# The last four up tiles of an MLP's first quarter as two seven-product pairs, with the sums of x made by ScalarE and GpSimd

## The chip, the core and the metric

One core of a Trainium2 chip runs the whole program. The metric is the device time of one execution in microseconds (us). The engines are named as in the profile: PE (TensorE, matrix products; PEld is its weight load), DVE (VectorE), ACT (ScalarE), POOL (GpSimd) and SP (SyncE, which here only issues DMAs). Each engine works through its instructions in order; semaphores tie the engines together.

## The reference

A two-layer encoder on 576 tokens (512 of a prompt, 64 of a running stream) with a model width of 1024. Layer 0 mixes tokens by causal pooling, layer 1 by sparse attention; each is followed by a squared-ReLU MLP.

```python
def _mlp(h, w_up, w_down):
    u = jax.nn.relu(h @ w_up)          # 1024 -> 4096
    return (u * u) @ w_down            # 4096 -> 1024
...
x = x + y                              # pooling or attention
x = x + _mlp(_rmsnorm(x, norm_mlp[i]), mlp_w_up[i], mlp_w_down[i])
```

## The kernel before, in words

Everything is fp32 to the reader of its output, but PE works on two-part numbers: a value is split into a high part (a cast by ACT to fp32r) and a low part (the difference, mostly by DVE), and a product is high·high + high·low + low·high, three matmuls. Activations lie as `x[k]`, k = 0 to 7, 128 features by 576 tokens each; a matmul takes one half of the tokens, 288 (`HT`).

**An MLP** (`mlp`, once for each layer) runs in four quarters c of the inner 4096 features. A quarter makes eight up tiles (1024 to 128 features each) and then four Down pairs, which add the quarter's part of the result to `x`. The norm's factor 1/rms isn't multiplied into the input: it is needed only where an up tile leaves PSUM (`rb`; the tile is called `rbm` in the first layer), so PE can begin before the norm is known. The steps of the norm: ACT squares `x[k]` (L343), DVE sums the squares (L344), PE sums over features (`st`), ACT and DVE make 1/rms with small steps (L396 to L403), DVE writes it on a diagonal (L366, L369), PE spreads it (`rb`, L356) and ACT copies it (L357). PE has the diagonal's two matmuls in the middle of plain tile 2.

**Plain tiles.** In the first quarter all eight up tiles are plain: `project` (L326) takes 48 matmuls for one, 8 k × 2 halves × 3, with two units of weights, `wh` and `wl` of 128x512 each. `finished` takes the tile out: DVE applies ReLU and `rbm` into the v tile (L480), ACT squares (L472), and then sums for the Down pairs' seven products are made (L502 to L515) and split into u, high by ACT (L491), low by DVE (L494). There is one v tile (`v_tile`, bufs=1).

**Seven-product pairs.** In the quarters 1 to 3 up tiles are made in pairs, `Up`, and Downs always are. `seven` computes a 2 by 2 block product with seven products instead of eight: products t1 to t4, b11, b21, b22 of 12 matmuls each (`product`, L528), 84 for two up tiles where plain ones would take 96. They go to three PSUM banks a, b and c in the order b11, t1, t2, b21, t3, b22, t4, and the scheduler may move some of them past another. `act.copy(a_, b)` (L565) copies b11 to a second bank. The products need sums of the weights (`sum`, by accumulating DMAs of POOL, L235 and L256, and by DVE, L281 and L285) and sums of x, called `xt`: three per j (t1, t2, t4), j = 0 to 3, each from `x[j]` and `x[half + j]`, and they need `xs[j]` replaced by a difference for `b22` and the like (`x_difference`).

**Sums of x before the change.** `x_sums(j, ...)` (L445) takes one ACT scaling of 128x288, four DVE operations of 128x288 (L451 to L454), an ACT cast and a DVE low part of 128x864. It is called after plain tile 3 for j = 0 and after tile 5 for j = 1; j = 2 and 3, and the `x_difference`s, come beside the first Downs (`x_prepared`).

**Weights.** `Stream` loads raw weights by SP's queue into a few raw tiles, in the order of the list `jobs`; a raw tile is loaded anew when the low part of what it held has been made. An "even" and an "odd" block belong to a pair; loading an odd one adds the even one to it by an accumulating DMA on POOL's queue. `units` yields split units one after another, and `ahead` sets how far it runs before PE.

**Seeds.** In the first four calls of `seven` of each MLP a further matmul writes `a_` before the copy overwrites it (`SEEDED`, L564). Nothing reads its result.

**The order of the instructions.** The code is written in the order of the work; a scheduler then fixes each engine's sequence, and within an engine nothing passes a waiting instruction. The changed kernel's line numbers are a little off those of before: L193/L194 are the same, L235, L256, L316, L326, L344, L357, L480 and L528 of before are L237, L258, L318, L328, L346, L359, L483 and L531.

Of the kernel before, what the change touches and what calls it, by code (L numbers as in the profile page):

```python
# [49 lines left out]
SPARE_UNITS = 6  # L50
RAWS = (4, 3)
MLP_BLOCKS = ("up", "even", "odd", "down")
SEEDED = 4
LEAD = 5
UP_ORDER = (0, 4, 1, 5, 2, 6, 3, 7)
FACTORS = ("t4", "t3", "t1", "t2", "b11", "b22", "b21")
FIRST_DOWN = (0, 2, 1, 3)

# [2 lines left out]
def pool_dsa_kernel(ctx: ExitStack, tc: tile.TileContext, a, o):  # L61
# [61 lines left out]
    def f32(t):  # L123
        return t.bitcast(F32)
# [37 lines left out]
    def mlp_jobs(layer, plain=0):  # L162
        for c in range(4):
            for n, f in enumerate(UP_ORDER):
                kind = "odd" if c and n % 2 else "even" if c else "up"
                jobs.append((kind, a["w_up"][layer, c * 8 + f], KT * P))
            for m in range(KT) if c else [2 * q + i for q in FIRST_DOWN for i in range(2)]:
                kind = "down" if c == 3 and m >= KT - plain else "odd" if m % 2 else "even"
                jobs.append((kind, a["w_down"][layer, c, m], KT * P))
# [27 lines left out]
    class Stream:  # L197
# [13 lines left out]
        def fill(self):  # L211
            while jobs:
                kind, src, n = jobs[0]
                mlp = kind in MLP_BLOCKS
                room = self.room(mlp)
                if room is None:
                    return
# [200 lines left out]
    def mlp(layer, gi, late=0, end=None):  # L418
# [23 lines left out]

            return (KT - LAST if end and c == 3 else KT) // 2

        def x_sums(j, raw, first, difference):  # L445

            t = x_sums_tile()
            xt.append(t)
            gain, minus = gv[:, gi, j:j + 1], negative[:, half + j:half + j + 1]
            act.activation(first, x[j][:, :HT], AF.Copy, scale=gain)  # L450
            dve.scalar_tensor_tensor(raw[:, 0], x[j][:, HT:], gain, first, ALU.mult, ALU.subtract)  # L451
            dve.scalar_tensor_tensor(difference, x[half + j][:, :HT], gv[:, gi, half + j:half + j + 1], first, ALU.mult, ALU.subtract)
            dve.scalar_tensor_tensor(raw[:, 1], x[half + j][:, :HT], minus, raw[:, 0], ALU.mult, ALU.subtract)
            dve.scalar_tensor_tensor(raw[:, 2], x[half + j][:, HT:], minus, raw[:, 1], ALU.mult, ALU.subtract)  # L454
            act.copy(t[:, :, 0], raw)
            dve.tensor_tensor(t[:, :, 1], raw, f32(t[:, :, 0]), ALU.subtract)

        def x_difference(j, difference):

            split(xs[j][:, :, :HT], difference)  # L460

        def of_x(j, factor, part):
            if factor[0] == "b" or factor == "t3":
# [32 lines left out]
        def parts_of(u, v, f):  # L496

            upper(u, v, f)
            return lower(u, v, f)
# [29 lines left out]
                                    skip_group_check=True)  # L529
            return ins  # L530

        tasks = [0]
        parted = []
        gates = []
        left = []
# [17 lines left out]
        def seven(operand, late, on):  # L553
# [5 lines left out]
            w = take()  # L559
            with behind([parted.pop()] if parted else []):  # L560
                product(b, w, operand, "b11", rows, True)
            tasks[0] += 1
            if tasks[0] <= SEEDED:
                pe.matmul(a_[:, :HT], w[0][:, :P], operand(0, "b11", 0), start=True, stop=True, skip_group_check=True)  # L564
            act.copy(a_[:, :HT], b[:, :HT])  # L565
            ahead()
            w1 = take()
# [143 lines left out]
        def finished(i, pt, us):  # L711
            nonlocal pair
            if i % 2 == 0:
                pair = tiles()
            v, u = pair
            activated(pt, v[:, 5:7] if i % 2 else v[:, 1:5:3])
            if i == KT - 2:
                parts_of(u, v, slice(4, 5))
                first_sum(v)
                parts_of(u, v, slice(2, 3))  # L720
            elif i == KT - 1:
                middle_sums(v)
                parts_of(u, v, slice(1, 4, 2))
                upper(u, v, slice(5, 7))
                last_sum(v)
                lower(u, v, slice(5, 7))
                parts_of(u, v, slice(0, 1))
            elif i % 2:
                upper(u, v, slice(4, 7))
                first_sum(v)  # L730
                middle_sums(v)
                last_sum(v)
                upper(u, v, slice(0, 4))
                lower(u, v, slice(4, 7))
                lower(u, v, slice(0, 4))
            if i % 2:
                us.append(u)

        todo, us = [], []
        for i in range(KT):  # L740
            w = next_block()
            pt = (psum1("up"), psum1("up")) if i == 2 else psum("up")
            project(pt, w, xs, spread() if i == 2 else iter(()))
            todo.append((i, pt, us))
            if i == 1:
                norm.stats()
            if i < 2:
                continue
            for t in todo:
                finished(*t)  # L750
            todo.clear()
            if i in (3, 5):
                r = 2 * i - 6
                if i == 3:
                    snap = halves(tmp("snap", "s2", 1))
                x_sums(i // 2 - 1, rough[:, r:r + 3], rough[:, r + 3], snap[:, i // 2 - 1])

        def x_prepared(n):

            if n < 2:  # L760
                v = v_tile()
                x_difference(n, snap[:, n])
                x_sums(n + 2, v[:, :3], v[:, 3], v[:, 4])
                x_difference(n + 2, v[:, 4])

        for n, q in enumerate(FIRST_DOWN):
            seven(of(us), n == 0, Down(q))
            x_prepared(n)
        for c in range(1, 4):
            us = []  # L770
            for j in range(half):
# [930 lines left out]
```

## Time and profile before

| | |
|---|---|
| median of three runs | 1071.51 us (1071.14 to 1071.96) |
| the profiled execution | 1070.67 us |
| its span, first to last instruction | 1068.8 us |
| mean granted clock of PE | 0.997 |
| busy: PE / DVE / ACT / POOL | 1046.4 / 912.0 / 625.7 / 239.5 us |
| layer 0, pooling and the plain tiles' start | plain tile 0 begins at 41.4 us |
| layer 1's MLP | its first tiles run at 680 us |

A row of the timeline gives the start, the duration, the engine, the line, the operation, what it writes and reads, its shape, how often it is repeated without a gap, and in brackets how long the engine was idle before it and what ended that. A row of groups gives the count, the busy time and the mean of one in ns, then the idle time before these instructions. A row of windows gives the busy time of PE, PEld, DVE, ACT and POOL with counts, then the clock, the DMA engines' share and GB/s. DVE's and ACT's instructions overlap a little, the next starting some 0.07 to 0.1 us before the last one's end.

### The profile page before, as it was taken

Reading aid. Unit: us, or ns where it says so; the run is one execution under the profiler, and the core shown is the slowest. Engines: PE = TensorE matmul, PEld = TensorE weight load, DVE = VectorE, ACT = ScalarE, POOL = GpSimd, SP = SyncE. Lnnn points to the kernel's source line nnn. Section 1 sums busy time; section 2 is a strip of 40 time slices with the busy share of each in tenths; the row PEclk is TensorE's granted clock in tenths of the full one; section 3 lists DMA queues with packets and bytes.
Section 4 is the critical chain, followed back from the end, with each engine's and each line's share of the span. In section 5 each row is a group of like instructions: output and inputs, shape, how many; then the busy total and the mean of one; then the engine's idle time right before and its main releaser. Section 6 shows DMA issues by size and latency. Waiting matters only on the chain.

```text
span 1068.8 us, 21707 instructions
## 1 busy us (share of the span) xinstructions
PE 1046.4 (98%) x7978; PEld 1022.7 (96%) x7978; DVE 912.0 (85%) x1865; ACT 625.7 (59%) x1252; POOL 239.5 (22%) x254
## 2 busy tenths in 40 slices
PE   8999999999999999999999999999999999999996
PEld 8999999999999999999999888999999999999995
DVE  7879989879988998889999675689889879979974
ACT  8556457547646765454368776456457447547742
POOL 3200111111111110667546620000111111111101
PEclk9999999999999999999999999999999999999998
DMA  8233666676576665845552554343666676676522
GB/s 254 89 102 92 165 165 163 158 179 156 151 182 169 157 173 176 237 137 139 170 156 75 169 170 107 126 107 89 178 159 149 178 172 164 149 183 163 124 55 89
DMA packets 98027, 159.65 MB, mean 149 GB/s; under 512 B 15697, under 2 KB 29312, under 8 KB 97920
## 3 DMA queue, kind: packets, MB, share of 16 engines
q1 hardware_dynamic: 70720, 111.78, 33.2%
q0 software_dynamic: 15840, 28.84, 17.1%
q10 hardware_dynamic: 11360, 17.63, 5.1%
q8 instruction: 63, 1.03, 0.4%
q14 instruction: 44, 0.36, 0.1%
HBM read 142.99 MB, written 12.72 MB: 146 GB/s over the span
## 4 chain that ended last, share of the span: by engine, by line
PE 84%; DVE 7%; DMA 3%; issue 2%; POOL 2%; ACT 1%; SPq 0%; ACTq 0%; DVEq 0%; POOLq 0%
PE b L528 33%; PE c L528 16%; PE up L326 9%; PE a L528 8%; PE pj L326 4%; PE wo L326 2%; PE wa L326 2%; PE pb L1072 1%; PE pt L1402 1%; PE dn L326 1%; PE o L1434 1%; DVE mask L1319 1%; PE sc L1376 1%; DVE m L1318 1%; DMA raw<-in_w_in 1%
## 5 line engine op out<-in xcount | busy, mean ns | idle before, releaser
L193 ACT CAST wh<-raw 128x512 fp32r<-128x512 f32 x308 | 189.7, 620 | 208.5 <-PE b L528 65.9
L194 DVE TENSOR_TENSOR wl<-raw,wh 128x512 fp32r<-128x512 f32 x284 | 198.2, 700 | 33.6 <-ACT wh L193 29.5
L528 PE MATMUL b<-u,wh 128*128 128x288 f32 x992 | 203.3, 296 | 2.3 <-ACT a L565 1.9
L528 PEld LDWEIGHTS b<-u,wh 128*128 128x128 f32 x992 | 159.6, 188 | 4.3 <-ACT a L565 3.1
L193 ACT CAST wh<-sum 128x512 fp32r<-128x512 f32 x165 | 102.3, 620 | 95.7 <-PE b L528 41.6
L528 PE MATMUL b<-u,wl 128*128 128x288 f32 x496 | 145.9, 295 | 0.4 <-DVE wl L194 0.4
L194 DVE TENSOR_TENSOR wl<-sum,wh 128x512 fp32r<-128x512 f32 x165 | 112.2, 686 | 22.3 <-ACT wh L193 20.8
L256 POOL DMA_DIRECT2D sum<-in_w_down x31 | 27.1, 894 | 340.9 <-DMA sum<-in_w_down 102.5
L528 PE MATMUL c<-u,wh 128*128 128x288 f32 x496 | 102.7, 296 | 0.0
L528 PEld LDWEIGHTS b<-u,wl 128*128 128x128 f32 x496 | 93.5, 189 | 0.6 <-DVE wl L194 0.6
L326 PE MATMUL up<-xs,wh 128*128 128x288 f32 x512 | 89.6, 296 | 0.9 <-DVE x L1593 0.8
L494 DVE TENSOR_TENSOR u<-v,u 128x576 fp32r<-128x576 f32 (+3 forms) x106 | 83.0, 786 | 2.0 <-ACT u L491 1.6
L528 PEld LDWEIGHTS c<-u,wh 128*128 128x128 f32 x496 | 79.8, 188 | 1.3 <-ACT wh L193 1.1
L528 PE MATMUL b<-xt,wh 128*128 128x288 f32 x384 | 77.7, 296 | 0.0
L528 PE MATMUL b<-xs,wh 128*128 128x288 f32 x384 | 77.2, 295 | 0.0
L326 PEld LDWEIGHTS up<-xs,wh 128*128 128x128 f32 x512 | 74.6, 188 | 2.0 <-ACT wh L193 1.0
L491 ACT CAST u<-v 128x576 fp32r<-128x576 f32 (+3 forms) x106 | 73.7, 699 | 3.2 <-DVE v L515 2.3
L528 PE MATMUL c<-u,wl 128*128 128x288 f32 x248 | 73.1, 295 | 0.0
L256 POOL DMA_DIRECT2D sum<-in_w_up x24 | 20.8, 865 | 203.1 <-DVE wl L194 83.4
L326 PE MATMUL pj<-xs,wh 128*128 128x288 f32 x352 | 62.1, 295 | 0.0
L528 PEld LDWEIGHTS b<-xt,wh 128*128 128x128 f32 x384 | 61.5, 188 | 0.0
L528 PEld LDWEIGHTS b<-xs,wh 128*128 128x128 f32 x384 | 61.2, 188 | 0.0
(300 smaller groups left out, 2724.7 us busy)
## 6 DMA issues: line engine op xcount, KB each, us to landing
raw<-in_w_up SPq DMA_DIRECT2D x128, 256.0 KB, 3.1
raw<-in_w_down SPq DMA_DIRECT2D x128, 256.0 KB, 2.9
raw<-in_w_o ACTq DMA_DIRECT2D x32, 256.0 KB, 2.8
sum<-in_w_down SPq DMA_DIRECT2D x31, 256.0 KB, 2.9
sum<-in_w_down POOLq DMA_DIRECT2D x31, 256.0 KB, 4.7
raw<-in_w_down POOLq DMA_DIRECT2D x31, 256.0 KB, 5.0
raw<-in_w_in ACTq DMA_DIRECT2D x30, 256.0 KB, 3.0
sum<-in_w_up SPq DMA_DIRECT2D x24, 256.0 KB, 3.2
```

Of the source, the lines that this page charges most:

```text
L193: cast(h, src)
L194: (sub or how["sub"]).tensor_tensor(l, src, f32(h), ALU.subtract)
L256: pool.dma_start(s1, odd[:, 512:], accum_op=ALU.add)
L326: pe.matmul(pt[h][:, :m] if isinstance(pt, tuple) else pt[:, h, :m], wt, xs[k][:, part, c:c + m], start=(k == 0 and i == 0), stop=(k == n ...
L491: return act.copy(u[:, f, 0], v[:, f])
L494: return dve.tensor_tensor(u[:, f, 1], v[:, f], f32(u[:, f, 0]), ALU.subtract)
L528: ins = pe.matmul(bank[:, :HT], wt, ut, start=first and j == 0 and i == 0, stop=j == 3 and i == 2, skip_group_check=True)
L1072: pe.matmul(pt[:, c0:c0 + rhs.shape[1]], lhs, rhs, start=n == 0, stop=n == len(steps) - 1)
L1318: dve.max(m8[rows], order[rows])
L1319: dve.match_replace(order[rows], m8[rows], order[rows], TAKEN)
L1376: pe.matmul(pt[:, hh, :nw], q[:, 2 * s + hh], ks[g][:, part, :nw], start=part == 0, stop=part == 1)
L1402: pe.transpose(pp[:, c:c + P], pr[:, hh, kt * P:(kt + 1) * P], ident)
```

## The change

Tiles 0 to 3 of a first quarter stay plain. Tiles 4 to 7 become the pairs `Up(0, 2)` and `Up(0, 3)`. For that all four sums of x are made during the plain tiles, one call of `x_sums` after each, and in another way: ACT scales `x[j]` and `x[half + j]` in full (128x576 each, the second with the negative gain), POOL makes four differences of 128x288, ACT casts (128x864) and POOL makes the low part (128x864). The four `x_difference`s (ACT and DVE) stand ahead of the Up pairs. The list of weights follows (the six blocks of two pairs with their sums, seven units for each pair, where two plain tiles had four), the seeds are gone, and the special cases of `finished` for tiles 6 and 7 go with them.

```diff
+PLAIN_UP = 4
-SEEDED = 4
 ...
-                kind = "odd" if c and n % 2 else "even" if c else "up"
+                kind = "up" if not c and n < PLAIN_UP else "odd" if n % 2 else "even"
 ...
+                if kind == "even" and "sums" not in phase:
+                    return
 ...
-        def x_sums(j, raw, first, difference):
+        def x_sums(j):
             t = x_sums_tile()
             xt.append(t)
-            gain, minus = gv[:, gi, j:j + 1], negative[:, half + j:half + j + 1]
-            act.activation(first, x[j][:, :HT], AF.Copy, scale=gain)
-            dve.scalar_tensor_tensor(raw[:, 0], x[j][:, HT:], gain, first, ALU.mult, ALU.subtract)
-            dve.scalar_tensor_tensor(difference, x[half + j][:, :HT], gv[:, gi, half + j:half + j + 1], first, ALU.mult, ALU.subtract)
-            dve.scalar_tensor_tensor(raw[:, 1], x[half + j][:, :HT], minus, raw[:, 0], ALU.mult, ALU.subtract)
-            dve.scalar_tensor_tensor(raw[:, 2], x[half + j][:, HT:], minus, raw[:, 1], ALU.mult, ALU.subtract)
-            act.copy(t[:, :, 0], raw)
-            dve.tensor_tensor(t[:, :, 1], raw, f32(t[:, :, 0]), ALU.subtract)
+            at = half * (1 + j % 2)
+            f = rough[:, at:at + 4]
+            for n, k, gain in ((0, j, gv[:, gi, j:j + 1]), (2, half + j, negative[:, half + j:half + j + 1])):
+                act.activation(f[:, n:n + 2].rearrange("p a t -> p (a t)"), x[k], AF.Copy, scale=gain)
+            pool.tensor_tensor(rough[:, j], f[:, 2], f[:, 0], ALU.add)
+            for n in range(1, 4):
+                pool.tensor_tensor(f[:, n], f[:, n], f[:, n - 1], ALU.subtract)
+            act.copy(t[:, :, 0], f[:, 1:])
+            pool.tensor_tensor(t[:, :, 1], f[:, 1:], f32(t[:, :, 0]), ALU.subtract)
 ...
-            tasks[0] += 1
-            if tasks[0] <= SEEDED:
-                pe.matmul(a_[:, :HT], w[0][:, :P], operand(0, "b11", 0), start=True, stop=True, skip_group_check=True)
 ...
-        for i in range(KT):
+        for i in range(PLAIN_UP):
             w = next_block()
             pt = (psum1("up"), psum1("up")) if i == 2 else psum("up")
             project(pt, w, xs, spread() if i == 2 else iter(()))
             todo.append((i, pt, us))
             if i == 1:
                 norm.stats()
 ...
+            x_sums(i)
+        snap = halves(tmp("snap", "s2", 1))
+        for j in range(half):
+            x_difference(j, rough[:, j])
+        for j in range(PLAIN_UP // 2, half):
+            up = Up(0, j)
+            seven(of_x, False, up)
+            us.append(up.u)
-        for n, q in enumerate(FIRST_DOWN):
-            seven(of(us), n == 0, Down(q))
-            x_prepared(n)
+        for q in FIRST_DOWN:
+            seven(of(us), q == FIRST_DOWN[0], Down(q))
```

Three places of layer 0's first quarter in the engines' sequences. POOL first: before, behind the low parts of the mixer's weights, it only issues DMAs for the MLP.

```order
L194 TENSOR_TENSOR wl_404<-raw_369,wh_403 128x512
L256 DMA sum_1220<-in_w_down 128x512
L235 DMA raw_920<-in_w_down 128x512
L235 DMA raw_1069<-in_w_down 128x512
L256 DMA sum_1418<-in_w_down 128x512
```

In the changed kernel (`rough` holds the scaled x and the differences, `xt` are the sums of x, `raw` and `sum` the weights):

```order
L457 TENSOR_TENSOR rough_676<-rough_676 128x288 x3
L459 TENSOR_TENSOR xt_726<-rough_676,xt_726 128x3x288
L459 TENSOR_TENSOR xt_834<-rough_676,xt_834 128x3x288
L237 DMA raw_762<-in_w_up 128x512
L457 TENSOR_TENSOR rough_676<-rough_676 128x288
L455 TENSOR_TENSOR rough_676<-rough_676 128x288
L457 TENSOR_TENSOR rough_676<-rough_676 128x288
L455 TENSOR_TENSOR rough_676<-rough_676 128x288
L457 TENSOR_TENSOR rough_676<-rough_676 128x288 x4
L459 TENSOR_TENSOR xt_933<-rough_676,xt_933 128x3x288
L459 TENSOR_TENSOR xt_1015<-rough_676,xt_1015 128x3x288
```

Twenty subtractions stand there now, and an accumulating DMA stands between the sums of j = 0, 1 and those of j = 2, 3; it waits for the raw tile's load by SP, which waits for DVE's `wl_759<-raw_377`, the low part of tile 3's second unit.

ACT next, around the copies to `rbm`. Before:

```order
L396 ACTIVATE rt_137_804<-st_797,eps 128x4
L396 ACTIVATE rt_137_804<-st_797,eps 64x1
L193 CAST wh_910<-raw_395 128x512
L357 COPY rbm_149_866<-rb_867 128x288
L357 COPY rbm_149_866<-rb_870 128x288
```

In the changed kernel (`wh` are weights, `negative` the negative gain):

```order
L454 ACTIVATE rough_676<-x_82,gv 128x576
L454 ACTIVATE rough_676<-x_84,negative_674 128x576
L398 ACTIVATE rt_140_821<-st_814,eps 128x4
L398 ACTIVATE rt_140_821<-st_814,eps 64x1
L193 CAST wh_942<-sum_843 128x512
L458 CAST xt_933<-rough_676 128x3x288
L359 COPY rbm_152_889<-rb_890 128x288
L359 COPY rbm_152_889<-rb_893 128x288
L458 CAST xt_1015<-rough_676 128x3x288
```

The cast of the third sum of x, which waits for POOL's seventh difference of the second set, now stands ahead of the two copies.

PE behind plain tile 2 (`up_855` and `up_856`), in the changed kernel; `up_956` is plain tile 3, `b_1035` bank b of the first Up pair:

```order
L328 MATMUL up_855<-xs_653,wl_396 128x288
L328 MATMUL up_856<-xs_653,wl_396 128x288
L531 MATMUL b_1035<-xs_632,wh_845 128x288 x2
L531 MATMUL b_1035<-xs_632,wl_846 128x288
...
L531 MATMUL b_1035<-xs_641,wl_846 128x288
L328 MATMUL up_956<-xs_632,wh_752 128x288 x4
...
L328 MATMUL up_956<-xs_653,wl_759 128x288 x2
L531 MATMUL b_1035<-xt_726,wh_942 128x288 x2
```

Where tile 3 followed tile 2 at once, the first product of the first Up pair (b11) now comes between them, and it waits for ACT's first copy to `rbm`; tile 3 waits, as before, for DVE's evacuation of tile 0, which needs both copies. Behind tile 3 stand t2, b21, t3, t1, the next pair's b11, b22 and t4.

More of the change, by code (lines that the diff above doesn't have):

```diff
@@ L443, in pairs @@
             return (KT - LAST if end and c == 3 else KT) // 2
-        def x_sums(j, raw, first, difference):
+        def x_sums(j):
             t = x_sums_tile()
             xt.append(t)
-            gain, minus = gv[:, gi, j:j + 1], negative[:, half + j:half + j + 1]
-            act.activation(first, x[j][:, :HT], AF.Copy, scale=gain)
-            dve.scalar_tensor_tensor(raw[:, 0], x[j][:, HT:], gain, first, ALU.mult, ALU.subtract)
-            dve.scalar_tensor_tensor(difference, x[half + j][:, :HT], gv[:, gi, half + j:half + j + 1], first, ALU.mult, ALU.subtract)
-            dve.scalar_tensor_tensor(raw[:, 1], x[half + j][:, :HT], minus, raw[:, 0], ALU.mult, ALU.subtract)
-            dve.scalar_tensor_tensor(raw[:, 2], x[half + j][:, HT:], minus, raw[:, 1], ALU.mult, ALU.subtract)
-            act.copy(t[:, :, 0], raw)
-            dve.tensor_tensor(t[:, :, 1], raw, f32(t[:, :, 0]), ALU.subtract)
+            at = half * (1 + j % 2)
[7 more added lines that the diff above has]
+            pool.tensor_tensor(t[:, :, 1], f[:, 1:], f32(t[:, :, 0]), ALU.subtract)
         def x_difference(j, difference):
-            split(xs[j][:, :, :HT], difference)
+            split(xs[j][:, :, :HT], difference, -1.0)
         def of_x(j, factor, part):
@@ L530, in product @@
             return ins
-        tasks = [0]
         parted = []
@@ L716, in finished @@
             activated(pt, v[:, 5:7] if i % 2 else v[:, 1:5:3])
[L717 to L728, printed above, removed]
+            if i % 2:
                 upper(u, v, slice(4, 7))
@@ L746, in mlp @@
                 norm.stats()
[L747 to L764, printed above, removed]
-        for n, q in enumerate(FIRST_DOWN):
-            seven(of(us), n == 0, Down(q))
-            x_prepared(n)
+            if i >= 2:
+                for t in todo:
+                    finished(*t)
+                todo.clear()
+            x_sums(i)
[8 more added lines that the diff above has]
+            seven(of(us), q == FIRST_DOWN[0], Down(q))
         for c in range(1, 4):
```

## The prediction

> **What bounds the kernel now.** The page comes first: its busy row and the chain that ended last.
>
> ```profile
> PE 1046.4 (98%) x7978; PEld 1022.7 (96%) x7978; DVE 912.0 (85%) x1865; ACT 625.7 (59%) x1252; POOL 239.5 (22%) x254
> PE 84%; DVE 7%; DMA 3%; issue 2%; POOL 2%; ACT 1%; SPq 0%; ACTq 0%; DVEq 0%; POOLq 0%
> ```
>
> PE is the bound over the whole: a matmul removed is time gained wherever PE is fed without a gap. But 85% for DVE is an average, so I read the stages of the change next: windows with the busy time of each engine (PE, PEld, DVE, ACT, POOL in this order). The first row is layer 0's plain tiles 0 to 3, the second what follows them (tiles 4 to 7), the third the same place of layer 1 as the first.
>
> ```profile
> 41.40:62.70 21.30, 21.30 (x159) 20.88 (x159) 14.11 (x26) 8.87 (x17) 0.89 (x1) 1.00 0.28 80
> 62.00:82.00 20.00, 19.92 (x151) 19.68 (x150) 19.26 (x34) 13.21 (x20) 1.19 (x2) 1.00 0.33 97
> 680.00:700.00 20.00, 20.00 (x149) 19.57 (x149) 7.29 (x16) 4.75 (x10) 0.86 (x1) 1.00 0.31 96
> ```
>
> PE has no gap in any of them, at full clock (1.00). DVE is busy 14.1 of 21.3 us in the first, all but full in the second (19.26 of 20.00), and light in the third. POOL has nothing to do but issue DMAs. So tiles 4 to 7 are PE's work with DVE just keeping up, and the change takes PE's work away there.
>
> The price of a matmul, from the timeline of PE:
>
> ```profile
> 47.80 0.43 PE L326 MATMUL up<-xs,wl 128*128 128x288 f32 x2
> 48.07 0.96 PE L326 MATMUL up<-xs,wh 128*128 128x288 f32 x6
> 48.86 0.29 PE L326 MATMUL up<-xs,wl 128*128 128x288 f32 x1
> ```
>
> From 47.80 to 48.86 eight are issued: 1.06 / 8 = 0.1325 us each.
>
> **What is removed.** Four plain tiles of 48 matmuls (192) become two pairs of 84 (168): −24 a layer, −3.2 us. The four seed matmuls a layer: −0.5 us. That is −7.4 us over both layers, if PE stays fed. The first Downs waited for the copy into the bank that the seed also wrote:
>
> ```profile
> PE b L528 <- ACT a L565: 1.0, 2, 0.5
> ```
>
> This row of the waits is of 41 to 135 us, and layer 1 answers with the same row. The seed stood between the copy's bank and PE, and DVE and ACT lose their sums of x from that stretch, so I let these waits go: −1.0 a layer, at most. Upper bound of the gain: 2 × (3.2 + 0.5 + 1.0) = 9.4 us.
>
> **What the sums of x cost on POOL.** Each j has four differences of 128x288 and one low part of 128x864. The groups of POOL:
>
> ```profile
> L824 POOL TENSOR_TENSOR x<-x,room 128x288 f32<-128x288 f32 x4 | 3.1, 797 | 42.7 <-ACT room L818 42.7
> L1176 POOL TENSOR_TENSOR rp<-rp,sn 128x576 f32<-128x576 f32 x4 | 5.8, 1438 | 0.0
> ```
>
> 288 more columns cost 0.64 us, so 864 are estimated at 1.438 + 0.64 = 2.08 us. Four j: 16 × 0.797 + 4 × 2.08 = 21.1 us of POOL a layer. Beside 21.3 us of plain tiles this would just fit, if POOL ran beside DVE. The trace has places that speak to this. The timelines of POOL and DVE in the attention, where both subtract tiles in SBUF:
>
> ```profile
> 442.52 1.76 POOL L1241 TENSOR_TENSOR cs<-cs,rba 128x576 f32<-128x576 f32 x1 [0.81 <-DMA qi<-qi]
> 444.24 1.68 POOL L1188 TENSOR_TENSOR st<-rp,st 128x448 fp32r<-128x448 f32 x1
> 455.84 1.44 POOL L1176 TENSOR_TENSOR rp<-rp,sn 128x576 f32<-128x576 f32 x1
> ```
>
> ```profile
> 442.91 1.98 DVE L1242 TENSOR_TENSOR sn<-sn,rba 128x576 f32<-128x576 f32 x1
> 445.37 1.10 DVE L194 TENSOR_TENSOR w<-raw,w 128x512 fp32r<-128x512 f32 x1 [0.47 <-ACT w L193]
> 455.89 1.93 DVE L194 TENSOR_TENSOR wl<-raw,wh 128x512 fp32r<-128x512 f32 x1
> 427.69 1.15 DVE L401 SCALAR_TENSOR_TENSOR nt<-r 128x5 f32<-128x5 f32 x1
> 28.64 0.82 DVE L1080 SCALAR_TENSOR_TENSOR x<-pb,gv,x 128x576 f32<-128x576 f32 x1 [0.89 <-PE pb L1072]
> ```
>
> L194 takes 0.69 us by its group (below); at 455.89 it took 1.93 and ended at 457.82, 0.54 after POOL's operation did. L1242 ended 0.62 after POOL's L1241, POOL's L1188 ended only after that, and the L194 at 445.37 ended 0.55 after L1188. They take turns, one whole instruction each. Even five columns (L401) took 1.15, against 0.17 where POOL is idle (below). The L1080 at 28.64, whose one tile is in PSUM, is at its usual 0.82 beside a POOL subtraction. The page "SBUF — State Buffer" of the Trainium skill ("Who interferes with whom") states the same rule: a DVE instruction with two SBUF inputs contends with a GpSimd instruction that reads SBUF, and the later one fully blocks; the trace agrees in the rows above. "Perfetto Trace Analysis" ("Optimizing Scalar/DVE Operations") draws from it that offloading from DVE to GpSimd might not help, which speaks against this change; by it the sum comes out as the walk below does, and by GpSimd's own time alone as the first rival.
>
> **Layer 0: rbm comes late.** DVE's groups from 41.4 to 64 us:
>
> ```profile
> L344 DVE TENSOR_TENSOR s<-s,xt 128x576 f32<-128x576 f32 x7 | 5.3, 756 | 0.3
> L194 DVE TENSOR_TENSOR wl<-raw,wh 128x512 fp32r<-128x512 f32 x6 | 4.1, 689 | 3.4 <-ACT wh L193 3.4
> L316 DVE SCALAR_TENSOR_TENSOR xs<-x,gv,xs 128x576 fp32r<-128x576 f32 x3 | 2.4, 813 | 0.0
> L366 DVE TENSOR_TENSOR xt<-ident,r 128x512 f32<-128x512 f32 x1 | 0.7, 691 | 0.0
> ```
>
> ```profile
> 44.74 0.77 ACT L315 ACTIVATE xs<-x,gv 128x576 fp32r<-128x576 f32 x1
> 61.36 0.88 ACT L357 COPY rbm<-rb 128x288 f32<-128x288 f32 x2 [2.07 <-PE rb L356]
> 64.63 0.92 ACT L491 CAST u<-v 128x864 fp32r<-128x864 f32 x1
> raw<-in_w_up SPq DMA_DIRECT2D x128, 256.0 KB, 3.1
> L235 POOL DMA_DIRECT2D raw<-in_w_up x24 | 22.8, 952 | 11.8 <-DVE wl L194 8.8 <-DVE u L494 1.7 <-DVE sum L281 1.0
> ```
>
> POOL can start behind ACT's first scalings (0.77 each, ahead of the last squares), at about 43.2. Its first set (j = 0, 1) is 8 × 0.80 + 2 × 2.08 = 10.5. In turns with it DVE has two xs lows, seven sums of squares and two weight lows: 1.6 + 5.3 + 1.4 = 8.3. Together 18.8, less some 0.08 for each of the 19 instructions that a neighbour's start covers: 17.4, to about 60.6. The last of these weight lows frees the raw tile into which the next weights are loaded (3.1, to 63.7); POOL's queue holds the accumulating DMA for that tile (0.95) ahead of the second set. So the second set starts at about 64.6. ACT is in order too: its cast of the third sum stands ahead of the copies to rbm. Seven differences (5.6) and some 1.4 of DVE's turns (the small steps of the norm, L366, a weight low) end at 71.6, the cast (0.92) at 72.5, the first copy at 72.9. PE's next product needs that at 62.6: **+10.0 us**. Without the turns the first set ends at 53.7, the DMA at 54.7, the second set's seventh difference at 60.3, and rbm comes in time: 0 is the low end. If DVE's turn goes ahead each time, some 12 is the high end. I take 10, since all the rows on the sharing say turns. PE's own waits for the late xs lows and for the sums of squares lie inside these 10.
>
> **Then the first Up pair waits for DVE.** Its last product, t4, takes the bank of t3, which DVE must first read into the v tile. There is one v tile, and it comes free when the plain tiles' u is split. After rbm DVE has in line: four tiles' evacuations 2.8, ten weight lows, two sums for weights, eight sums of v, the lows of two u (864 and 1152 columns each), four lows of differences of x.
>
> ```profile
> 62.27 1.42 DVE L480 SCALAR_TENSOR_TENSOR v<-up,rbm 128x576 f32<-128x576 f32 x2 [2.26 <-ACT rbm L357]
> 64.21 0.45 DVE L502 TENSOR_TENSOR v<-v 128x288 f32<-128x288 f32 x1
> 64.77 0.46 DVE L509 SCALAR_TENSOR_TENSOR v<-v 128x288 f32<-128x288 f32 x1
> 65.88 1.05 DVE L494 TENSOR_TENSOR u<-v,u 128x864 fp32r<-128x864 f32 x1
> ```
>
> 2.8 + 12 × 0.69 + 12 × 0.45 + 2 × 1.05 + 2 × 1.35 (the 1152, estimated from 0.45 and 1.05) = 21.3; with 0.08 overlap each, 19.1. PE from rbm to that product has that pair's first product, tile 3, and five more of the pair's and one of the next pair's products ahead of t4: 12 + 48 + 72 = 132 matmuls, 17.5. So PE waits between 1.6 and 3.8; I take 2.8, and 0 where ACT or the idle time ahead has let DVE work forward. The six further weight splits a layer lie in this line; ACT's part has room (13.2 of 20 in the window).
>
> Layer 0: +10.0 + 2.8 − 3.2 − 0.5 − 1.0 = **+8.1 us**.
>
> **Layer 1.** DVE is light ahead of rbm, so POOL's first set runs nearly alone. But the second set hangs on the same raw tile, whose weight low waits for PE:
>
> ```profile
> 686.29 0.69 DVE L194 TENSOR_TENSOR wl<-raw,wh 128x512 fp32r<-128x512 f32 x1 [2.48 <-ACT wh L193]
> 694.15 0.17 DVE L401 SCALAR_TENSOR_TENSOR nt<-r 128x5 f32<-128x5 f32 x1
> 699.20 0.88 ACT L357 COPY rbm<-rb 128x288 f32<-128x288 f32 x2 [2.06 <-PE rb L356]
> ```
>
> 687.0 + 3.1 + 0.95 = 691; seven differences with the norm's small steps between them (5.6 + 1.4) to 698; cast to 699. The copy was at 699.2 before, so the norm's own steps, each up to 0.8 late, decide: 0 to +2; I take +1. Then the same 2.8: +1.0 + 2.8 − 3.2 − 0.5 − 1.0 = **−0.9 us**.
>
> **Sum.** 1070.67 (the profiled execution: its span of 1068.8 and 1.87 around it) + 8.1 − 0.9 = 1077.9. The median of the runs shown is 1071.51, 0.84 above that execution: 1078.7, rounded 1079.
>
> **The rivals.** About 0.2%, 2.1 us, is what a measurement of this kernel can tell from no change.
>
> 1. *POOL runs beside DVE, or its backlog is absorbed* (faster). rbm in time in both layers, DVE's line covered by idle time: down to −9.4, 1062; with 1.6 of stall in each, −6.2, 1065. For it: POOL's 21.1 us fit into 21.3 without turns, and PE is at 98%. Against it: every row of two SBUF readers that met. The point that decides is 60 to 62 us: the second set's seventh difference ends before PE needs rbm. With two or three us of lateness it is still faster (about 1068). Chance 0.25.
> 2. *The gain is eaten by the v tile alone* (no change). rbm in time, but 3.8 of stall in each layer and the L565 waits stay: 2 × (3.8 − 3.7) = 0, 1071.5 ± 2. Also reached when rbm is some 4 us late in one layer and the rest goes well. Chance 0.13.
> 3. *As forecast*: rbm late in layer 0 by 6 to 12. 1074 to 1086. Chance 0.50.
> 4. *Layer 1 pays too*: its second set finds the norm's steps and the weights as DVE's turns and rbm is 8 late there as well, 1087 or more. For it: the chain is the same. Against it: 7.29 us of DVE in 20. Chance 0.12.
>
> That the change does not remove what it says is excluded by the order: PE has 24 matmuls and four seeds fewer in each layer.
>
> **How the numbers follow.** Likeliest is the third, 1079, its own range 1074 to 1086. The range of 8 in 10 leaves out the best of the first (0.10) and most of the fourth (0.10): 1065 to 1087. Faster by over 0.2%: 0.26; within: 0.13; slower: 0.61.
>
> **What would show it.** Right: POOL differences of 1.1 to 1.6 us instead of 0.80 at 43 to 60 us and sums of squares above 0.76; the cast of the third sum near 72 and rbm right after it; PE idle some 10 us in sum before tile 3, on rbm and the last xs; about 3 us ahead of t4 of the first Up pair, released by DVE. Wrong: differences at 0.80 beside DVE's lows at their usual times, rbm at 62, PE without a gap to 85.

## The result, and the profile after

The changed kernel takes 1083.31 us (median of four runs, 1081.85 to 1084.17) beside 1071.74 (1071.14 to 1073.13) for the kernel before: ratio 1.0105, interval 1.0093 to 1.0118. That is 11.6 us slower; 7.5 had been forecast. Its profiled execution took 1084.17 us, with a span of 1082.4 and a mean granted clock of 0.988. It is the slowest of the four, and that of the kernel before (1070.67) is a quick one, so the two traces read below are 13.5 us apart, not 11.6.

First the page of the changed kernel, the busy row and the chain:

```profile
PE 1048.8 (97%) x7922; PEld 1024.0 (95%) x7922; DVE 934.7 (86%) x1863; ACT 643.1 (59%) x1296; POOL 292.4 (27%) x302
PE 79%; DVE 10%; issue 3%; POOL 3%; ACT 2%; DMA 2%; SPq 0%; ACTq 0%; DVEq 0%; POOLq 0%
```

PE has 56 matmuls fewer, as counted, and yet is busy 2.4 us longer, so some of its matmuls became slower. DVE has two instructions fewer and is busy 22.7 us longer. POOL's 48 new instructions took 52.9.

The windows of the changed kernel say where. The first two rows are the stretches shown of before, the third is the first Up pairs of layer 0, the last two are layer 1's plain tiles and its first Up pairs:

```profile
41.40:62.70 21.30, 20.39 (x151) 19.72 (x151) 20.57 (x25) 14.11 (x24) 15.44 (x12) 1.00 0.12 38
62.00:82.00 20.00, 14.25 (x88) 13.54 (x88) 19.80 (x21) 9.51 (x18) 11.35 (x11) 0.83 0.20 54
82.00:105.00 23.00, 20.02 (x139) 19.79 (x138) 21.21 (x40) 16.09 (x31) 3.45 (x4) 0.93 0.54 126
689.00:709.00 20.00, 17.55 (x122) 17.10 (x121) 11.90 (x8) 10.22 (x18) 17.10 (x19) 0.91 0.39 90
733.00:745.00 12.00, 8.80 (x46) 8.56 (x46) 10.63 (x20) 7.22 (x14) 0.86 (x1) 0.72 0.44 111
```

In the second row DVE is "busy" 19.80 of 20 us with 21 instructions, where before it did 34 in 19.26: its instructions stand. PE did 88 matmuls instead of 151, and the granted clock is 0.83. The clock is below 1.00 in layer 1 too, and no term of the forecast had that.

PE's waits in the changed kernel, first 41 to 135 us, then 680 to 760:

```profile
PE rb L358 <- DVE xt L371: 5.7, 1, 5.7
PE b L531 <- DVE v L668: 3.0, 1, 3.0
PE up L328 <- DVE xs L318: 0.9, 2, 0.7
```

```profile
PE b L531 <- DVE v L668: 3.2, 1, 3.2
PE up L328 <- DVE xs L318: 2.5, 1, 2.5
PE rb L358 <- DVE xt L368: 1.3, 1, 1.3
...
```

The first row is the diagonal of 1/rms, and L668 is DVE's step ahead of t4. The waits for the copy to bank a are gone.

The heart of it stands in the timelines of the changed kernel, POOL first, then DVE, ACT and PE:

```profile
43.54 0.88 POOL L457 TENSOR_TENSOR rough<-rough 128x288 f32<-128x288 f32 x1 [8.30 <-ACT rough L454]
44.39 1.31 POOL L455 TENSOR_TENSOR rough<-rough 128x288 f32<-128x288 f32 x1
...
62.03 0.88 POOL L237 DMA_DIRECT2D raw<-in_w_up  x1 [3.65 <-DVE r L405]
62.65 1.09 POOL L457 TENSOR_TENSOR rough<-rough 128x288 f32<-128x288 f32 x1
...
65.65 3.28 POOL L457 TENSOR_TENSOR rough<-rough 128x288 f32<-128x288 f32 x4
```

```profile
43.00 5.90 DVE L346 TENSOR_TENSOR s<-s,xt 128x576 f32<-128x576 f32 x5
...
61.80 0.69 DVE L368 TENSOR_TENSOR xt<-ident,r 128x512 f32<-128x512 f32 x1
62.40 6.58 DVE L371 TENSOR_SCALAR xt<-ident,r 128x64 f32<-128x64 f32 x1
```

```profile
68.21 0.91 ACT L458 CAST xt<-rough 128x864 fp32r<-128x864 f32 x1 [7.55 <-POOL rough L457]
69.03 0.39 ACT L359 COPY rbm<-rb 128x288 f32<-128x288 f32 x1
70.47 0.40 ACT L359 COPY rbm<-rb 128x288 f32<-128x288 f32 x1 [1.05 <-PE rb L358]
```

```profile
69.13 1.30 PE L358 MATMUL rb<-xt,ones 128*128 128x288 f32 x2 [5.75 <-DVE xt L371]
71.19 0.68 PE L531 MATMUL b<-xs,wh 128*128 128x288 f32 x2
71.67 0.44 PE L531 MATMUL b<-xs,wl 128*128 128x288 f32 x1
73.98 0.70 PE L328 MATMUL up<-xs,wh 128*128 128x288 f32 x4
```

In the first set (43 to 60 us) DVE and POOL take turns: five sums of squares in 5.90 us, 1.18 each, and a POOL difference of 1.31. In the second set they do not. Eight differences follow each other every 0.75 us from 62.65 on, and one DVE instruction of 64 columns is shown from 62.40 to 68.98: it ends when the last of the eight does, at 68.93. PE sat 5.75 us in front of the diagonal. From 69.13 its matmuls are issued every 0.24 us (71.19 to 71.67 is two) instead of 0.13.

Sums by place, from the starts of matmuls in the two timelines. Plain tile 0 begins at 41.4 before and 41.3 after, the attention's first projection at 409.0 and 418.2: layer 0 costs +9.3. The last matmul starts at 1058.5 and 1074.9, which leaves +7.1 for layer 1 (6.9 in its MLP, 0.2 in its attention). The span ends 10.3 us behind that start before, and 7.5 after: −2.8. Together +13.6, the difference of the two spans.

### The profile page after: what moved, and what is told of

The parts are those of the page before. It is cut to its first block, busy times and chain, and to the rows that moved or that the text cites. A ratio compares the mean times of both kernels' runs of the same rounds, so it can differ in the third digit from the quotient of the medians.

```text
span 1082.4 us, 21752 instructions
## 1 busy us (share of the span) xinstructions
PE 1048.8 (97%) x7922; PEld 1024.0 (95%) x7922; DVE 934.7 (86%) x1863; ACT 643.1 (59%) x1296; POOL 292.4 (27%) x302
## 4 chain that ended last, share of the span: by engine, by line
PE 79%; DVE 10%; issue 3%; POOL 3%; ACT 2%; DMA 2%; SPq 0%; ACTq 0%; DVEq 0%; POOLq 0%
PE b L531 35%; PE c L531 17%; PE a L531 9%; PE pj L328 4%; PE wo L328 3%; PE wa L328 2%; PE up L328 2%; DVE wl L194 1%; PE pt L1383 1%; PE dn L328 1%; PE o L1415 1%; DVE mask L1300 1%; PE sc L1357 1%; DVE m L1299 1%; PE pb L1053 1%
## 5 line engine op out<-in xcount | busy, mean ns | idle before, releaser
L193 ACT CAST wh<-sum 128x512 fp32r<-128x512 f32 x177 | 109.6, 619 | 102.0 <-PE b L531 46.2
L194 DVE TENSOR_TENSOR wl<-sum,wh 128x512 fp32r<-128x512 f32 x177 | 124.3, 708 | 27.6 <-ACT wh L193 26.0
L531 PE MATMUL b<-xt,wh 128*128 128x288 f32 x448 | 92.3, 300 | 6.2 <-DVE v L668 6.2
L531 PE MATMUL b<-xs,wh 128*128 128x288 f32 x448 | 91.4, 297 | 0.0
L497 DVE TENSOR_TENSOR u<-v,u 128x576 fp32r<-128x576 f32 (+2 forms) x108 | 83.4, 773 | 2.9 <-ACT u L494 2.2
L531 PEld LDWEIGHTS b<-xt,wh 128*128 128x128 f32 x448 | 72.9, 191 | 6.7 <-DVE v L668 6.7
L494 ACT CAST u<-v 128x576 fp32r<-128x576 f32 (+2 forms) x108 | 74.2, 689 | 3.6 <-DVE v L518 1.9
L531 PEld LDWEIGHTS b<-xs,wh 128*128 128x128 f32 x448 | 72.4, 190 | 0.2 <-ACT rbm L359 0.2
L531 PE MATMUL b<-xt,wl 128*128 128x288 f32 x224 | 66.9, 298 | 0.0
L531 PE MATMUL b<-xs,wl 128*128 128x288 f32 x224 | 64.7, 297 | 0.0
```

The costliest lines, as they stand in the source:

```text
L193: cast(h, src)
L194: (sub or how["sub"]).tensor_tensor(l, src, f32(h), ALU.subtract)
L494: return act.copy(u[:, f, 0], v[:, f])
L497: return dve.tensor_tensor(u[:, f, 1], v[:, f], f32(u[:, f, 0]), ALU.subtract)
L531: ins = pe.matmul(bank[:, :HT], wt, ut, start=first and j == 0 and i == 0, stop=j == 3 and i == 2, skip_group_check=True)
```

## The experiments

**Which part of the change costs?** Three kernels undo or isolate parts.

*POOL's subtractions alone.* The kernel before, with 20 subtractions on POOL added in each MLP, on tiles of x, of the change's shapes. Nothing reads their results, so the computation is that of before. ACT's scalings for the old sums of j = 0, 1 are besides held behind an earlier cast of u, which moves some of ACT's and DVE's instructions a few places back; three later kernels of this kind have the same hold, and the one with tiny subtractions (below) is no slower for it: 1068.53 us beside 1069.4 without hold and subtractions.

```diff
+            if i < half:
+                for n in range(4):
+                    pool.tensor_tensor(rough[:, 8 + n], x[i][:, :HT], x[half + i][:, :HT], ALU.subtract)
+                pool.tensor_tensor(rough[:, 11:14], rough[:, 8:11], rough[:, 8:11], ALU.subtract)
 ...
+            with behind(cast if j < 2 else []):
+                act.activation(first, x[j][:, :HT], AF.Copy, scale=gain)
```

> The kernel before, with nothing but 20 subtractions of POOL more in each MLP (4 of 128x288 and one of 128x864 for each of four j, on tiles of x; their results are not read). Theory (POOL's subtractions keep DVE's two-input instructions out): POOL runs from about 42 to 63 us in layer 0 and from 680 to 700 in layer 1, DVE's sums of squares and lows wait for it, PE waits some 10 us in layer 0 and 5 or more in layer 1, and the clock falls after it: 1085 to 1098 us. Rival (the loss comes from ACT's order or from the chain of the sums itself, and POOL runs beside DVE): within 1 us of before, 1071 to 1073, with DVE's rows at their usual durations.

Measured: 1082.49 us, ratio 1.0087 (1.0066 to 1.0109). Work that nobody waits for costs 10.5 us, less than the 13 or more that were expected. PE's waits in this kernel, 41 to 140 us:

```profile
PE up L326 <- DVE v L481: 2.4, 1, 2.4
PE up L326 <- DVE xs L316: 1.6, 1, 1.6
PE st L376 <- DVE s L344: 1.3, 1, 1.3
PE b L529 <- ACT a L566: 1.0, 2, 0.5
...
```

The first three are DVE's. So rival 1, POOL beside DVE, is refuted. The fourth, the copy into the seed's bank, stays, since the seeds stay.

*The same sums by DVE.* The changed kernel with `pool` replaced by `dve` in `x_sums`:

```diff
-            pool.tensor_tensor(rough[:, j], f[:, 2], f[:, 0], ALU.add)
+            dve.tensor_tensor(rough[:, j], f[:, 2], f[:, 0], ALU.add)
 ...
-            pool.tensor_tensor(t[:, :, 1], f[:, 1:], f32(t[:, :, 0]), ALU.subtract)
+            dve.tensor_tensor(t[:, :, 1], f[:, 1:], f32(t[:, :, 0]), ALU.subtract)
```

> The changed kernel with all of POOL's subtractions of the sums of x given to DVE. Theory (the loss ahead of rbm is POOL keeping DVE out, not the work itself): DVE has 12 to 13 us more of its own a layer (16 of 0.45 and 4 of 1.05 to 1.15) instead of waiting 21; in layer 1, where DVE had 12.7 us idle ahead of rbm, the 2.8 us on the last xs and the half clock behind it go; in layer 0 rb is 2 to 5 us late instead of 6.2. The stall before t4 (3.2 a layer) and its half clock stay: 1074 to 1079. Rival (POOL beside DVE is cheaper than the work on DVE): slower than the changed kernel, over 1084.

Measured: 1071.14 us, 0.9985 (0.9974 to 0.9995), better than expected and 12.2 below the changed kernel. The windows of this kernel:

```profile
62.00:82.00 20.00, 18.18 (x122) 17.39 (x121) 17.89 (x34) 14.99 (x26) 1.71 (x2) 0.91 0.30 79
689.00:709.00 20.00, 20.00 (x148) 19.44 (x147) 16.04 (x36) 12.54 (x25) 0.85 (x1) 1.00 0.26 67
```

With 40 instructions more DVE is less busy over the span than beside POOL's sums (924.5 us against 934.7). The price is small: DVE's groups in layer 0 have 450 ns for a difference and 1048 for a low part, 7.2 + 4.2 = 11.4 us for 16 and 4, where POOL's groups have 27.0 us for the same and hold DVE up meanwhile. What is left of PE's waits, from 41 to 135 us, then from 680 to 770:

```profile
PE rb L358 <- DVE xt L368: 1.8, 1, 1.8
PE b L531 <- DVE v L668: 1.4, 1, 1.4
...
```

```profile
PE b L531 <- DVE v L668: 3.9, 1, 3.9
...
```

The xs wait of layer 1 is gone and the one at the diagonal is 1.8 instead of 5.7; the stall ahead of t4, which is DVE's own line, stays.

*No seeds.* The kernel before with one line changed; only matmuls are left out that nothing reads.

```diff
-SEEDED = 4
+SEEDED = 0
```

> The kernel before without the eight seed matmuls, and nothing else of the change. Theory (they cost their pitch): 8 x 0.13 = 1.1 us less, 1070 to 1071; the two waits of 0.5 us on the copy in each layer's first Downs are still there unless the scheduler orders the Downs otherwise. Rival (the seeds gave the copy's bank an early owner and so kept the order of the first Downs): 0 to 2 us slower than before, with waits on the copy as long or longer.

Measured: 1069.4 us, 0.997 (0.9959 to 0.9982). There is no PE wait at all from 41 to 140 us. The waits on the copy to bank a go with the seeds; relief of DVE has no part in it. Each MLP is 1.4 us shorter, about what the sum had for seeds and copy (0.5 and 1.0).

From these, at the start of the last matmul: no seeds −1.6 (1058.5 to 1056.9), two pairs with sums by DVE +3.7 (to 1060.6), those sums by POOL +14.3 (to 1074.9). So even without POOL the two pairs don't pay: 48 matmuls fewer, 6.4 us, and the last one still 3.7 later (2.3 and 1.9 in the two MLPs). The medians agree: 1071.14 beside 1069.4, although the program's end is 2.8 us shorter with the pairs.

**Can the lateness be routed around?** Three kernels treat what the first trace showed: the diagonal's 64 columns standing on DVE, and the cast of the third sum standing ahead of ACT's copies to `rbm`. The first gives the 64 columns to ACT, the second has the casts of the third and fourth sum follow the copies, the third does both.

```diff
 ...
+            act.activation(diag[:, c * block:n], ident[:, :rest], AF.Copy, scale=r[:, c:])
 ...
```

```diff
-            act.copy(t[:, :, 0], f[:, 1:])
+            with behind([norm.copied.ins] if j > 1 else []):
+                act.copy(t[:, :, 0], f[:, 1:])
```

> The changed kernel, with the last 64 columns of the diagonal (L371, 6.58 us in the changed kernel's layer 0) written by ACT. Theory (two locks in series: the diagonal's tail on DVE, and behind it ACT's cast of the third sum, which waits for POOL until 68.2): the copies to rbm come right behind that cast at 69 and 69.4 instead of 69.0 and 70.5, PE goes on some 1.3 us sooner in layer 0, nothing in layer 1: 1081 to 1082.5. Rival (the tail on DVE is the whole loss): rbm at 63, 8 us gained in layer 0, 1075.

> The changed kernel, with ACT's casts of the third and fourth sum held behind its copies to rbm. Theory (two locks in series): the diagonal's tail still ends at 68.9, so the copies are at 69.5 and 70.5 as before and the cast moves from 68.2 to about 71: 0 to +1.5, 1083 to 1085. Rival (ACT's order is the whole loss): rbm at 63, 8 us gained in layer 0, 1075.

> The changed kernel with both: the diagonal's tail by ACT and the casts of the third and fourth sum behind the copies to rbm. Theory (two locks in series): rb at 63, rbm at 64, tile 3 follows, the gap of 6.2 us in layer 0 and the half clock behind it (some 2 us) are gone; some 1 to 3 us come back where t2 waits for the sums whose casts and lows are later. Layer 1 stays. 1075 to 1078. Rival (either alone is the cause): as good as the one of the two that gains.

Measured: 1083.12 (1.0101, 1.0086 to 1.0116), 1086.95 (1.0144, 1.0122 to 1.0167) and 1088.33 (1.015, 1.0133 to 1.0168). The first moved the copies to 69.3 and 69.6 us, as expected, and the time stayed; the other two came out above what was expected. My theory of two locks in series, which open together, fell: with both treated the time should have dropped by 5 us or more, and it rose by 5. The timelines of the kernel with both, DVE and then ACT:

```profile
62.30 0.69 DVE L368 TENSOR_TENSOR xt<-ident,r 128x512 f32<-128x512 f32 x1
63.25 6.78 DVE L194 TENSOR_TENSOR wl<-sum,wh 128x512 fp32r<-128x512 f32 x1 [0.26 <-ACT wh L193]
```

```profile
63.92 0.89 ACT L359 COPY rbm<-rb 128x288 f32<-128x288 f32 x2 [0.76 <-PE rb L358]
```

`rbm` is there at 63.92, as intended, and DVE still doesn't move: now its next weight low stands for 6.78 us, and behind it is the evacuation that tile 3 waits for. This kernel's PE waits from 41 to 135 us:

```profile
PE up L328 <- DVE v L486: 6.7, 1, 6.7
PE b L534 <- DVE v L671: 3.9, 1, 3.9
...
```

What is lost is not one late result but DVE's whole time during POOL's set, whatever is first in its line; with the tail alone by ACT it was the same weight low, for 6.82 us. And the casts moved back make DVE's and PE's later work wait: the stall ahead of t4 went from 3.0 to 3.9 here, and to 4.9 where the casts alone were moved.

**Why turns in one set and none in the other?** In the second set an accumulating DMA is issued by POOL just ahead of the differences. So: POOL's unread subtractions once more, with one unread DMA issue of POOL ahead of the third j's.

```diff
+                if i == 2:
+                  with behind([low.ins]):
+                    pool.dma_start(rough[:, 6:8].rearrange("p a t -> p (a t)")[:, :512], a["w_up"][layer, 0][:, :512])
```

> The kernel before with POOL's 20 subtractions alone, and one DMA issue on POOL's queue between the second and the third j of each layer. Theory (behind a DMA issue POOL's instructions are started before the one ahead has ended, and then DVE gets no turn until the run ends; without one the two take turns): the four subtractions behind the DMA take 3.0 us together instead of 4.9, and one instruction of DVE stands for 3 us or more there; the total within 2 us of the run without the DMA, 1080 to 1085. Rival (what let no DVE instruction in was that each subtraction of the changed kernel waits for the one before): turns as without the DMA, no DVE instruction over 2.6 us.

Measured: 1082.78 us, 1.0098 (1.0084 to 1.0112). POOL's timeline in the kernel without that DMA, then in the one with it:

```profile
56.21 4.88 POOL L750 TENSOR_TENSOR rough<-x,x 128x288 f32<-128x288 f32 x4
```

```profile
55.67 0.61 POOL L751 DMA_DIRECT2D rough<-in_w_up  x1
56.30 3.04 POOL L753 TENSOR_TENSOR rough<-x,x 128x288 f32<-128x288 f32 x4
```

With turns four differences take 4.88 us; behind a DMA issue 3.04, and the sum of squares of DVE beside them took 3.59. So a DMA issue ahead of the run does take DVE's turns away, and it does so though these subtractions don't wait for one another: the rival falls. The total is that of the kernel without it (1082.49): who goes first changes which PE wait shows up (here 3.7 us for the sums of squares, in one piece), not the time.

**What does the half clock cost?** The changed kernel with 36 matmuls, whose result nothing reads, in layer 0's gap behind the diagonal.

```diff
+                for _ in range(n if h else 0):
+                    pe.matmul(pb[:, :HT], w, u, start=True, stop=True)
```

> The changed kernel with 36 more matmuls in layer 0, on the second rb bank ahead of the real one (their result is overwritten): they run in the gap of 6.2 us that PE has there anyway. Theory (a gap of 2.7 us or more makes the clock fall to half for some 4 us afterwards, which costs as much again): the clock stays at 1.00 between 66 and 74 us, the matmuls behind the gap keep their pitch of 0.13, and the time falls by 1.5 to 2.5 us: 1081 to 1082. Rival (PE is slow there because it waits for operands): no change, or longer by what of the 36 x 0.13 = 4.8 us doesn't fit.

Measured: 1086.26 us, 1.0131 (1.0117 to 1.0145). Its window, beside the changed kernel's:

```profile
70.00:72.00 2.00, 2.00 (x17) 1.98 (x15) 1.64 (x1) 1.89 (x4) 2.00 (x2) 1.00 0.05 12
```

```profile
70.00:72.00 2.00, 2.00 (x9) 1.86 (x9) 2.00 (x2) 1.53 (x3) 1.72 (x2) 0.50 0.01 4
```

The clock stayed at 1.00 and tile 3 began at 72.83 instead of 73.98. But the stall ahead of t4 grew from 3.0 to 4.3 us, and t4 came at 93.30 instead of 93.03: DVE's line sets that place, so the half clock of this gap cost nothing, and the expected 1081 to 1082 was wrong. Layer 0 ends at 418.4, where the changed kernel's ends at 418.2. The rest of the loss, some 2.5 us, arose in the attention, which is unchanged; its cause stays open. In the fourteen profiles the attention takes between 270.2 us (before) and 273.0 (this kernel), so 2 us between two totals need not come from the edit itself.

**What would be better?** One pair instead of two (tiles 6 and 7), sums by DVE, made behind tiles 0 to 3, or, in a second kernel, behind tiles 2 to 5.

```diff
-PLAIN_UP = 4
+PLAIN_UP = 6
 ...
-            x_sums(i)
+            if i < half:
+                x_sums(i)
```

```diff
+            if i > 1:
+                x_sums(i - 2)
```

> Sums of x by DVE as in the run that gave them to DVE, and only the last two up tiles of each first quarter as a pair (six plain tiles), so 12 matmuls fewer in each layer than plain, not 24; no seeds. Theory (what limits the pairs is DVE's line between rbm and t4; two more plain tiles give DVE 12.7 us more of PE's time, for three weight lows less): the stall before t4 is under 1 us in both layers and the clock stays up: 1067 to 1070, 0 to 2 us below the kernel before without seeds (1069.4). Rival (DVE's sums ahead of rbm cost more than the pair gains): 1070 to 1073, with the gaps at rb.

> As the run with six plain tiles and DVE's sums, but each sum of x two tiles later (after tiles 2 to 5, so behind the norm). Theory (DVE is full behind rbm and has room ahead of it): rb is in time in both layers, but DVE's line behind rbm is 12 us longer and the stall before t4 is 3 us or more with half a clock behind it: 1070 to 1075. Rival (the norm's lateness is what counts, DVE keeps up behind it): 1067 to 1069, better than with the sums ahead.

Measured: 1066.16 us (0.9947, 0.9933 to 0.9961), faster than before; and 1077.0 (1.0042, 1.0029 to 1.0055), above what was expected. The early sums run where DVE has room, beside a plain stretch of which 14.1 of 21.3 us are used; the late ones stand in the line that is full, and PE waits for them. PE's waits from 41 to 140 us, first with early, then with late sums:

```profile
PE up L328 <- DVE v L483: 1.3, 1, 1.3
PE st L378 <- DVE s L346: 0.3, 1, 0.3
...
```

```profile
PE c L531 <- DVE xt L459: 1.9, 2, 1.4
PE c L531 <- ACT snap L653: 1.0, 1, 1.0
```

But the faster one's last matmul is at 1058.0, and that of the kernel without seeds is at 1056.9: it wins at the end, where its span is 7.7 us behind the last matmul's start instead of 10.3. Of the 3.2 us between the two medians (1066.16 and 1069.4) 2.6 are this end, so the pair itself is about even.

**What makes the end shorter?** POOL's last drain differs, and with it the number of DMAs that POOL issues: 110 before, 118 after. Two kernels without seeds or pairs: one with four unread DMA loads on POOL's queue, one with eight tiny subtractions instead. PE, ACT and DVE have the same instructions in the same order in both.

```diff
+            if i < 2:
+                pool.dma_start(rough[:, 8 + 2 * i:10 + 2 * i].rearrange("p a t -> p (a t)")[:, :512], a["w_up"][layer, i][:, :512])
```

```diff
+            if i < 4:
+                pool.tensor_tensor(rough[:, 8 + i, :8], x[i][:, :8], x[i][:, 8:16], ALU.subtract)
```

> The kernel before without seeds, with four more DMA issues of POOL (plain loads of 128x512 that nothing reads), so 114 instead of 110 on its queue. It asks why POOL's last drain takes 8.5 us in the kernel before and 2.65 in the changed one, so that the program of before ends 2.8 us later behind its last matmul. Theory (it depends on POOL's DMAs: 110 and 112 gave 8.5 and 8.6, 118 gave 2.65, 114 gave 2.33): the drain takes 2.3 to 2.7 us, and the span ends 7.1 to 7.7 us behind the last matmul instead of 9.9 to 10.3. Rival (it depends on something else, as on the number of POOL's instructions): 8.5.

> The kernel before without seeds, with eight more subtractions of POOL on 8 columns (nothing reads them), so 8 more instructions and no more DMAs. Theory (the last drain depends on POOL's DMAs): 8.5 us as before. Rival (it depends on where POOL's last instructions lie, 467 to 468 and 516 to 518 gave 8.5, 474, 487 and 532 gave 2.3 to 2.65): 2.3 to 2.7 us at 475.

Measured: 1064.29 us (0.9926, 0.9902 to 0.995), the fastest of all kernels here, and 1068.53 (0.9965, 0.9953 to 0.9978). The drain's line (shortest, median and longest in ns) of before, of the changed kernel, of the kernel with four DMAs and of the one with tiny subtractions:

```profile
L1686 POOLq DRAIN  x3: 40/102/8493, 1059.4 to 1068.4; - x3
```

```profile
L1667 POOLq DRAIN  x3: 40/102/2649, 1075.8 to 1082.1; - x3
```

```profile
L1689 POOLq DRAIN  x3: 46/102/4407, 1056.5 to 1062.2; - x3
```

```profile
L1689 POOLq DRAIN  x3: 46/93/8485, 1057.5 to 1066.5; - x3
```

In all fourteen profiles POOL's longest drain is 8.5 us with 110 DMAs of POOL, 8.6 with 112, 2.3 or 4.4 with 114 and 2.65 with 118. It goes with the DMAs, not with subtractions, but since 114 gave two values, the number alone doesn't set it; by what mechanism was not settled. The kernel with four DMAs ends 6.9 us behind its last matmul's start, the one with tiny subtractions 10.2. A further 1.0 us between these two, whose last matmuls start at 1055.6 and 1056.6, isn't explained either.

## Why the prediction was right in sign and short in size

**Right.** The matmuls: 56 fewer at 0.1325 us. The price of a difference on POOL (0.75 us apart, 0.80 expected) and of a low part (2.02 where it is alone, 2.08 expected). The turns in the first set. The stall ahead of t4: 2.8 forecast for each layer, 3.0 and 3.2 measured. Layer 0 as a whole: +8.1 forecast, +9.3 measured. The walk to +10.0 is slightly off by its own figures: 72.9 against 62.6 is 10.3, and 19 overlaps of 0.08 make 17.3, not 17.4.

**Layer 0, right for a partly wrong reason.** The second set began at 62.65, not at 64.6, and gave DVE no turns: its eight differences took 6.3 us, and DVE's small steps had been done before. The first product behind `rbm` came at 71.19 instead of 62.6, 8.6 late, where 10.0 stood in the sum; the cast of the third sum, the sign that was to show the mechanism, came at 68.21 instead of near 72. The page "SBUF — State Buffer" of the Trainium skill ("Who interferes with whom") has the later instruction fully blocked for the whole of the earlier; the runs agree, and show besides that the block can last a whole run of POOL instructions when that run follows a DMA issue. What the term lacked is what follows the gap: seen from the matmuls' starts, PE's gaps grew by 10.1 us in layer 0, the half clock added 2.6, and 28 fewer matmuls gave 3.7 back; 10.1 + 2.6 − 3.7 = 9.0, of 9.3 measured.

**The step that failed: layer 1.** "DVE is light ahead of rbm, so POOL's first set runs nearly alone", hence +1 for rbm and −0.9 in all. Measured: +7.1. DVE is light there, but what it does is on PE's path at once, and here DMA issues of POOL stand ahead of all but one difference of the first set (at 690.39) and ahead of the second (at 703.39). The timelines of the changed kernel, POOL, DVE and ACT:

```profile
690.39 0.86 POOL L237 DMA_DIRECT2D raw<-in_w_up  x1
691.00 1.09 POOL L455 TENSOR_TENSOR rough<-rough 128x288 f32<-128x288 f32 x1
```

```profile
691.71 5.51 DVE L318 SCALAR_TENSOR_TENSOR xs<-x,gv,xs 128x576 fp32r<-128x576 f32 x1 [1.95 <-ACT xs L317]
706.26 4.66 DVE L194 TENSOR_TENSOR wl<-sum,wh 128x512 fp32r<-128x512 f32 x1 [2.27 <-ACT wh L193]
```

```profile
715.49 0.88 ACT L359 COPY rbm<-rb 128x288 f32<-128x288 f32 x2 [1.58 <-PE rb L358]
```

One low part of xs, usually 0.8 us, stood 5.51 behind a run that follows a DMA issue, and PE waited 2.5 for it; beside the second set a weight low stood 4.66; then PE waited 1.3 for the diagonal and 3.2 ahead of t4. The copies to `rbm` began 26.9 us behind layer 1's first tile (at 688.64) instead of 20.0 before (679.21 to 699.20): 6.9 late, where the sum has 1. PE's gaps grew by 6.3 in all, the half clock added 4.2, the matmuls gave 3.7 back: 6.8, of 7.1 measured. Rival 4, layer 1 paying too, had this right (rbm 8 late there as well). Its time of 1087 or more is what the profiled execution would have come to, 1087.0 (the median 1086.1), if the end had not become 2.8 us shorter for a reason that nobody forecast. So the sign was right because of layer 0, but that the time lies inside the third rival's range is partly luck.

**Terms missing.** The clock: gaps of 6.2 and 3.3 us between matmul starts in layer 0 and of 2.75 and 3.5 in layer 1 were each followed by a granted clock of 0.50, for 3.4 us (twice) or 6.8 (twice), beginning 2.6 to 4.6 us behind the gap's start; after one of 1.6 it didn't fall. "TensorE: Matmul & The Clock Gate" of the Trainium skill (Part 1) gives an idle window of about 3.4 us for that. The stretches here are one or two such windows long, but the runs show no such threshold for a single gap: 2.11 us (the sums by DVE, clock 0.50 from 64.9) and 2.28 (POOL's subtractions with the DMA, from 689.7) were enough, while 2.76 and 3.27 (the tail by ACT, at 693 and 89 us) were followed by a clock of 1.00. By pitch the half clock added 6.8 us to PE in the two layers, but the run with unread matmuls shows that such a sum is no loss where DVE sets the end. The other is the drain, −2.8. **The term put in part to a wrong cause:** the waits of 1.0 a layer on the copy to bank a did go, but with the seeds alone, not by any relief of DVE and ACT.

Why one DVE instruction can be shut out through several of POOL's behind a DMA issue, and not otherwise, is not explained; that it happens is shown. It was not tried to move the accumulating DMA to another place of POOL's queue in the changed kernel.

## What to carry to other kernels

An engine that is idle by the page is free only if its instructions don't shut out those of the engine that is full, as POOL's did DVE's here: add its work to the old kernel, unread, and see whether that is free, before building on it. When a stall is moved from one instruction to the next without any gain, the resource is what is late, not the result. After every gap of a few microseconds that a change opens on PE, look at the granted clock too, and look at the end of the program separately from its work.

## What the runs showed of the hardware

- DVE with two SBUF operands beside POOL: one for one in turns (0.75 became 1.18 to 1.36 us), but shut out through a whole run of POOL's behind a DMA issue (5.51 us beside seven differences, 6.78 beside eight, 3.59 beside four). A 64-column tensor_scalar of DVE with its operands in SBUF was shut out as well (6.58).
- POOL's last drain went with the DMAs that POOL issued: 8.5 us with 110 and 8.6 with 112, 2.3 or 4.4 with 114, 2.65 with 118. Four loads that nothing reads made a kernel 4.2 us faster than eight tiny subtractions in their place (1064.29 and 1068.53), 3.3 of it at the end.
- The granted clock fell to 0.50 in stretches of 3.4 us or a small multiple (6.8 in the changed kernel). A gap of 2.11 us between matmuls was followed by one; a gap of 3.27, in another kernel, wasn't.
